# Squares added by VectorE, two query products between the output projection's last jobs, and one paced list for the weight and inner sums

## The chip, the cores and the metric

The kernel runs on one core of a Trainium2 chip. The metric is the device time of one execution in microseconds (us), median of the runs. The core's engines are PE (TensorE, matrix products), DVE (VectorE), ACT (ScalarE), POOL (GpSimd) and SP (SyncE, which here only issues transfers). ACT and POOL issue transfers as well. Each engine works through its own instructions in order and waits on semaphores for the others.

## The reference

One decoder layer on 1024 tokens of width 1024: a state-space branch and an mLSTM branch, merged by gates and projected; cross-attention into 256 memory tokens; a ConvFFN; a final norm. Cut to what the change touches:

```python
merged = g_s5 * (y_s5 @ w_br_s5) + g_m * (y_m @ w_br_m)
x = x + merged @ w_out                                   # output projection
h = _rmsnorm(x, x_norm_g)                                # needs the squares of x
x = x + _cross_attn(h, _rmsnorm(mem, mem_norm_g), wq, wkv, wo)
h = _rmsnorm(x, f_norm_g)
u = _causal_dwconv(h @ w_up, conv_w, conv_b)             # up projection, 1024 -> 2 x 2816
a, b = split(u, 2)
x = x + (gelu(a) * b) @ w_down
return _rmsnorm(x, final_norm_g)
```

## The kernel before

**Products.** Activations lie with channels on the partitions. Every float32 product is made of three matmuls on a high and a low part of each operand (high x high, high x low, low x high). A weight tile is loaded by SP into a raw buffer, cast to its high part by ACT (L187) and subtracted to its low part by DVE (L188); `load_w` (L193) does this. The raw buffers WR and the parts WH and WL have two buffers each.

**Seven products for eight.** The gates, output, query, up and down projections are cut into 2 x 2 blocks and done with seven block products (numbered 1 to 7) in place of eight, by Winograd's form of Strassen's method. Some of the seven need sums of weight blocks. These are made in DRAM by transfers that POOL issues, half of them plain copies and half with an adding write: `quad_sums` (L982) yields eight transfers for a piece (512 KB each, smaller ones for the odd last piece of the down weights). The weight sums are Gw (gates), Ow (output), Qw (query), Uq (first eight pairs of the up projection) and Dd (down). They stand in one list, `slow_sums`, 120 entries in this order. `next_sum` (L210) issues the next one and makes it wait for the latest matmul (`last_mm`); `sums_on` sets how often a call does so: 0 never, 1 at each call, n when the argument is a multiple of n. The down projection also needs sums of the inner activations, Td from Gq, 40 entries, which `hidden_sums` (L1555) issues eight at a time as soon as pairs 8, 10, 12, 15 and 17 are finished, the first four of each eight waiting for the latest up product.

**Stages around the change.** First come the branches and gates, in an order written by hand (`ORDER`, L51), where `SUMS_OFF` and `SUMS_HALF` name the steps with no sums or half of them. The output projection has 14 jobs (`ojobs`, L1028): block products 1, 2, 3, 6, 7, 5, 4, each for two column groups. `out_job` (L1076) asks for the next job's weights, for the residual of the job after it, does 24 matmuls, calls `next_sum`, and empties PSUM; `out_x` (L1057) makes the new x from a result, its split for the query product, its squares on ACT, and adds them to `sq1` on POOL (L1069). No sums are issued in this stage, since `sums_on` is 0. The residual of jobs 12 and 13 comes by loads of POOL, the second of each adding (L1052, L1053).

The query stage follows a list (`QKV`, L62): j is a query product (14 of them, `q_job`, L1190, 24 matmuls), k a tile of keys, v a step of the values, s and t sums and splits of x for later query products, x the norm of x, a the first scores. Query products 0 and 1 need only the parts of x that output jobs 2 and 3 make; 2 and 3 need those of jobs 10 and 11, 4 and 5 those of jobs 12 and 13. Products 12 and 13 are kept for the attention (`Q_LATE`).

The attention has eight units (two token halves, four heads): scores, softmax, transposes, values (L1699 to L1716). From unit 4 on the tiles of the product with w_o run in between. Its first weight tile is asked for in unit 4. Some of the softmax tiles take WR buffers (L1309).

The up projection has 154 jobs of 12 matmuls (L1668, L1669): for pairs 0 to 7 first products 1 and 2 (jobs 0 to 15), then five each (jobs 16 to 55), then seven for each of pairs 8 to 21. Pairs 0 to 7 load sums from Uq, Y tiles of 256 KB; later pairs load two halves of 512 KB (`in_w_up`, L1479) and add the blocks on DVE (L1483). A finished pair goes through convolution and gelu, and is stored in Gq or Gd. The down projection has 63 jobs of 12 matmuls, and then a last part for the last four pairs.

**Order.** The program text gives priorities; a planner puts the instructions of each engine in order by a simulated timeline, so that an instruction may stand ahead of others that are earlier in the text. On the chip each engine keeps the order that was planned.

Of the kernel before, what the change touches and what calls it, by code (L numbers as in the profile page):

```python
# [15 lines left out]
ALU = mybir.AluOpType  # L16
# [4 lines left out]
P = 128  # L21
T = 1024
D = 1024
KD = D // P
# [29 lines left out]
).split()  # L54
NG = 2
SUMS_OFF = "p2 r1 g0 l2 y0 a1 l3 r2 r3 e10 e11 e20 e21 e30 e31 e60".split()
SUMS_HALF = ("a0", "a2", "a3", "a4")

Q_SUM = range(14)
Q_LATE = {0: 12, 2: 13}  # L60
V_FROM = 1
QKV = (  # L62
    "j0 s0 j1 k0 s1 v0 s2 j2 s3 k1 v1 t60 j3 t61 k2 t62 v2 t63 j4 x0 k3 t70 v3 t71 j5 k4 t72 v4 t73 j6 k5 t40 v5 t41 j7 t42 k6 v6 t43 j8 k7 v7 t50 j9 t51 t52 t53 j10 j11 a0 a1 "
).split()

COLS = {}
# [25 lines left out]
def hybrid_layer(ctx: ExitStack, tc: tile.TileContext, a):  # L92
    nc = tc.nc
# [963 lines left out]
    def out_x(n, h, u, ps):  # L1057
        i, odd = n // 2, n % 2
        x = qraw[i, odd, h] = Y() if odd or h else qe0[i // 2][:, H[i % 2]]
        V.tensor_tensor(out=x, in0=u, in1=ps, op=ALU.add)  # L1060
        if odd or not h:
            t = (S if odd else VV)(F32R)
            qp[1 + odd + odd * h, i] = scaled_split(x, col("x_g", n) if odd == h else nxg[:, n : n + 1], t[:, H[0]], t[:, H[1]])
        if fresh_sq[h]:
            A.activation(out=sq1[h], in_=x, func=AF.Square)
        else:
            t = Y()
            A.activation(out=t, in_=x, func=AF.Square)
            G.tensor_tensor(out=sq1[h], in0=sq1[h], in1=t, op=ALU.add)  # L1069
        fresh_sq[h] = False  # L1070
        A.dma_start(out=X1d[n][:, H[h]], in_=x)

# [2 lines left out]

    def out_job(k):  # L1076
        p, g = ojobs[k]
        out_weights(k + 1)
        out_resid(k + 2)
        wh, wl = ows.pop((p, g))  # L1080
        if p != 2:
# [196 lines left out]
    for k, (p, g) in enumerate(ojobs):  # L1278
        if k in (1, 2):
            out_sums(2 * k - 2)  # L1280
        if k in OUT_TURNS:
            out_turn(OUT_TURNS[k])
        if k == MEM_AT:
            mem_parts()
        out_job(k)

    r2s = cp.tile([P, 8], F32, name="r2s")
    r2n = cp.tile([P, 8], F32, name="r2n")
# [99 lines left out]
            nc.sync.dma_start(out=t, in_=X1d[n])  # L1388
            x1.append(t)

    def o_load(n):
        ow.append(load_w(a["w_o"][n % KD], (KD, P)))

    def o_tile(half, n):
        hs = H[half]
# [157 lines left out]
    Td = dr.tile([NPP, P, 4, T], F32, name="Td")  # L1553

    def hidden_sums(jj):  # L1555
        for i, (out, in_, kw) in enumerate(quad_sums(Td, Gq, jj, (1, 3, 3, 2), (0, 1, 0, 2), both_of(jj), range(8))):
            d = nc.gpsimd.dma_start(out=out, in_=in_, **kw)
            if i < 4:
                tc.add_manual_dep(d.ins, up_mm[0].ins.name, DependencyInfo(DependencyClass.Sync, DependencyReason.DATA), reason="pace")

    up_mm = [None]

# [134 lines left out]
    turned = None  # L1697
    sums_on[0] = 1
    for u in range(len(units)):  # L1699
        if u == 4:  # L1700
            o_load(0)
            x1_load(0)
            x1_load(1)
        probs(u + 1, 0)
        if u in Q_LATE:
            q_job(Q_LATE[u])
        elif u < 4:
            next_sum()
        t_ = att_turn(pes.pop(u))
        first_half(2 * (u - 5) + 1)  # L1710
        probs(u + 1, 1)
        if u:
            att_values(*units[u - 1], turned)
            next_sum()
        turned = t_
        first_half(2 * (u - 4))  # L1716
    first_half(KD - 1)
    att_values(*units[-1], turned)
    for n in range(KD):
        if n < KD - 1:  # L1720
            o_load(n + 1)
        o_tile(1, n)
        if n < 6:
            next_sum()
        if n == 1:
            pb = o_norm(0)
# [48 lines left out]
        put(4, i, xo[:, H0], S)  # L1775
    for i in range(4):
        put(3, i, x1[2 * i + 1][:, H1], S)
    raws, ops, wraws = [iter(range(len(djobs))) for _ in range(3)]
    for k in range(2 * NE, len(jobs)):
        up_job(k)  # L1780
        i = k - (len(jobs) - 7)
        if i >= 0:
# [18 lines left out]
    gs, ws = [], []  # L1801
    for k in range(len(djobs)):
        down_job(k)
        down_wraw(next(wraws, len(djobs)))
        down_w(k + 7)
        down_raw(next(raws, len(djobs)))
# [179 lines left out]
```

## Time and profile before

| | us |
|---|---|
| median of three runs | 1617.1 |
| lowest, highest | 1613.93, 1621.98 |
| the profiled execution | 1621.01 |
| its span, first to last instruction | 1619.2 |

PE's granted clock was 0.991 of full speed in the mean. The chain of work that ended last, followed back from the last instruction, by engine:

| engine or wait | share of the span |
|---|---|
| PE | 79% |
| DVE | 8% |
| DMA | 7% |
| ACT | 4% |
| issue | 2% |

How to read it: a row of the timeline with [idle <- releaser] gives how long the engine stood before this instruction and what it waited for last. Matmuls are pipelined: the duration of one overlaps the next. The share of busy time is a mean over stages with different limits, so stages are read one by one, in windows. In rows of the windows the last three numbers are the granted clock, the busy share of the 16 DMA engines and GB/s.

The stages in the profiled execution: output projection to about 680 us, query stage to about 800, attention and product with w_o to about 950, up projection to 1388, down projection after it.

### The profile page before, as it was taken

The page shows a single profiled execution, that of the slowest core. Times are in us where ns is not written, and L with a number is a line of the kernel's source. Part 1 is how long each engine was busy: PE and PEld are TensorE (multiplying, and loading weights), DVE is VectorE, ACT ScalarE, POOL GpSimd, SP SyncE. Part 2 cuts the span into 40 slices and gives each one's busy share as a digit, 9 for nine tenths or more (in the row PEclk, how much of TensorE's full clock was granted, in tenths as well). Part 3 has the DMA queues.
Part 4 walks back from the last instruction along what each step waited for, and adds up shares of the span by engine and source line. Part 5 has one row for each costly group of instructions (what it writes and reads, how often), then busy time and mean ns, then how long its engine had stood idle before and what let it go on. Part 6 is the DMA issues. An engine that isn't in the chain of part 4 may idle for free.

```text
span 1619.2 us, 21148 instructions
## 1 busy us (share of the span) xinstructions
PE 1575.9 (97%) x7887; PEld 1323.6 (82%) x7887; DVE 1168.5 (72%) x1844; ACT 772.6 (48%) x1261; POOL 206.8 (13%) x288
## 2 busy tenths in 40 slices
PE   9999999999999999899989999999989999999997
PEld 7898888888888787788878877888877888888887
DVE  7878767675565897957676558789877978967535
ACT  6446555633564447644454336444443444643413
POOL 1001111000101102410010100000121011221014
PEclk9999999999999999999999999999999999999998
DMA  6255645645986667565475568754797466876312
GB/s 200 94 148 136 157 118 126 149 98 143 294 300 179 147 156 227 176 205 175 106 225 147 168 184 267 202 153 127 213 228 181 123 176 200 310 262 207 119 39 105
DMA packets 104391, 282.09 MB, mean 174 GB/s; under 512 B 11488, under 2 KB 25504, under 8 KB 104288
## 3 DMA queue, kind: packets, MB, share of 16 engines
q1 hardware_dynamic: 67456, 163.90, 30.3%
q0 software_dynamic: 29296, 102.51, 28.1%
q10 hardware_dynamic: 7536, 14.33, 2.3%
q8 instruction: 62, 1.02, 0.3%
q14 instruction: 41, 0.34, 0.1%
HBM read 245.57 MB, written 114.82 MB: 223 GB/s over the span
## 4 chain that ended last, share of the span: by engine, by line
PE 79%; DVE 8%; DMA 7%; ACT 4%; issue 2%; POOL 0%; ACTq 0%; POOLq 0%; SPq 0%; DVEq 0%
PE M L223 25%; PE A L1505 11%; PE M L1505 9%; PE M L1652 6%; PE A L1652 5%; PE A L895 4%; PE M L1200 4%; PE A L223 2%; DMA S<-in_w_up_dram 2%; PE A L1267 1%; PE M L310 1%; DMA WR<-in_w_uq_dram 1%; PE A L1372 1%; DVE WL L188 1%; ACT S L187 1%
## 5 line engine op out<-in xcount | busy, mean ns | idle before, releaser
L223 PE MATMUL M<-S,WH 128*128 128x512 f32 (+1 forms) x1160 | 312.2, 380 | 5.8 <-ACT WH L187 4.0
L223 PEld LDWEIGHTS M<-S,WH 128*128 128x128 f32 x1160 | 211.6, 189 | 45.8 <-ACT WH L187 4.6
L187 ACT CAST WH<-WR 128x1024 fp32r<-128x1024 f32 (+2 forms) x113 | 107.4, 950 | 223.0 <-PE M L223 83.8
L223 PE MATMUL M<-S,WL 128*128 128x512 f32 (+1 forms) x580 | 184.3, 378 | 1.3 <-DVE WL L188 1.3
L188 DVE TENSOR_TENSOR WL<-WR,WH 128x1024 fp32r<-128x1024 f32 (+2 forms) x113 | 126.1, 1116 | 47.6 <-ACT WH L187 46.4
L223 PEld LDWEIGHTS M<-S,WL 128*128 128x128 f32 x580 | 109.1, 189 | 21.6 <-DVE WL L188 2.2
L1505 PE MATMUL M<-S,Y 128*128 128x512 f32 x468 | 111.9, 389 | 0.0
L1505 PEld LDWEIGHTS M<-S,Y 128*128 128x128 f32 x468 | 87.8, 188 | 18.5 <-DVE Z L1518 0.3
L1528 DVE SCALAR_TENSOR_TENSOR S<-Z,cols,S 128x1023 f32<-128x1023 f32 (+1 forms) x72 | 90.6, 1278 | 7.8 <-ACT S L1526 7.6
L1505 PE MATMUL M<-S,W 128*128 128x512 f32 x324 | 78.3, 389 | 0.0
L187 ACT CAST W<-Y 128x512 fp32r<-128x512 f32 x51 | 31.4, 619 | 85.8 <-PE A L1505 62.0
L1505 PE MATMUL A<-S,W 128*128 128x512 f32 x288 | 70.9, 389 | 0.7 <-ACT W L187 0.7
L1505 PEld LDWEIGHTS M<-S,W 128*128 128x128 f32 x324 | 60.8, 188 | 12.6
L1092 PE MATMUL A<-S,WH 128*128 128x512 f32 x224 | 69.0, 396 | 1.2 <-ACT A L1086 0.7
L895 PE MATMUL A<-S,WH 128*128 128x512 f32 x224 | 67.2, 390 | 0.0
L1505 PE MATMUL A<-R,W 128*128 128x512 f32 x228 | 58.3, 400 | 7.1 <-ACT Z L1512 7.1
L1505 PEld LDWEIGHTS A<-S,W 128*128 128x128 f32 x288 | 54.0, 188 | 12.2 <-ACT W L187 1.1
L1505 PE MATMUL A<-S,Y 128*128 128x512 f32 x240 | 59.9, 389 | 0.0
L188 DVE TENSOR_TENSOR S<-S,S 128x512 fp32r<-128x512 f32 x79 | 52.3, 685 | 9.8 <-ACT S L187 9.6
L1200 PE MATMUL M<-S,WH 128*128 128x512 f32 x192 | 59.3, 390 | 0.0
L1505 PEld LDWEIGHTS A<-R,W 128*128 128x128 f32 x228 | 43.6, 192 | 17.6 <-ACT Z L1512 8.4
L1652 PE MATMUL M<-S,W 128*128 128x512 f32 x240 | 57.7, 389 | 0.0
(528 smaller groups left out, 3594.4 us busy)
## 6 DMA issues: line engine op xcount, KB each, us to landing
Uq<-in_w_uq_dram POOLq DMA_DIRECT2D x24, 512.0 KB, 4.9
Dd<-in_w_dq_dram POOLq DMA_DIRECT2D x24, 512.0 KB, 5.8
Td<-Gq POOLq DMA_DIRECT2D x24, 512.0 KB, 8.1
WR<-in_w_in_dram SPq DMA_DIRECT2D x21, 512.0 KB, 4.3
Gq<-S SPq DMA_DIRECT2D x18, 512.0 KB, 4.3
WR<-in_w_o_dram SPq DMA_DIRECT2D x16, 512.0 KB, 4.5
Y<-Uq SPq DMA_DIRECT2D x32, 256.0 KB, 5.2
S<-Td POOLq DMA_DIRECT2D x16, 512.0 KB, 5.3
```

Of the source, the lines that this page charges most:

```text
L187: A.copy(out=hi, in_=src)
L188: (lo_eng or V).tensor_tensor(out=lo, in0=src, in1=hi.bitcast(F32), op=ALU.subtract)
L223: last_mm[0] = PE.matmul(ps[:, s:e], lhsT, rhs[:, s:e], start=first and is_first, stop=last and is_last)
L310: PE.matmul(pus[j][h.start // 512], w_[:, 0, j * P : (j + 1) * P], x_[:, h], start=k == 0 and f, stop=k == KD - 1 and l)
L895: last_mm[0] = PE.matmul(ps[q], w[:, 0, c], x, start=f, stop=l, skip_group_check=True)
L1092: last_mm[0] = PE.matmul(ps[q], w[:, 0, c], x, start=f, stop=l, skip_group_check=True)
L1200: last_mm[0] = PE.matmul(ps[q], w[:, 0, c], x, start=f, stop=l)
L1267: PE.matmul(pv[2 * m + j], lhsT, rhs[:, 0, 512 * j : 512 * j + 512], start=k == 0 and f, stop=k == KD - 1 and l)
L1372: last_mm[0] = PE.matmul(po, lhsT[:, ns], rhs, start=f, stop=l)
L1505: up_mm[0] = PE.matmul(ps, lhsT[:, c], rhs, start=f, stop=l, skip_group_check=True)
L1528: V.scalar_tensor_tensor(out=acc[:, d_:], in0=raw[:, : T - d_], scalar=col("fcw", 3 * ct + 2 - d_), in1=acc[:, d_:], op0=ALU.mult, op1=ALU ...
L1652: paced[0] = PE.matmul(dps[p][n], lhsT[:, c], rhs, start=f, stop=l, skip_group_check=True)
```

## The change

Six things are edited. (1) The squares of x are added by VectorE instead of GpSimd. (2) Query products 0 and 1 are moved from the head of the query list to between output jobs 11, 12 and 13; their weights are asked for in jobs 11 and 12 (`OUT_Q`), and value weights are asked for from the first step of the query stage on. (3) One sum is issued in every odd output job (and by the second of the moved products), two more in gate tiles a2 and a3, fewer in the attention's second half and beside the product with w_o. (4) Query product 12 runs in unit 1 of the attention, not in unit 0. (5) The first weight tile of w_o is asked for in unit 3, into a Z buffer in place of a WR buffer. (6) The inner sums go to the end of `slow_sums`, and the up projection issues one sum every fourth job before job 28 and one every second job from there on; the down jobs would issue what is left.

```diff
-SUMS_HALF = ("a0", "a2", "a3", "a4")
+SUMS_HALF = ("a0", "a4")
 
 Q_SUM = range(14)
-Q_LATE = {0: 12, 2: 13}
-V_FROM = 1
+Q_LATE = {1: 12, 2: 13}
+V_FROM = -1
+OUT_Q = {11: 0, 12: 1}
 QKV = (
-    "j0 s0 j1 k0 s1 v0 s2 j2 s3 k1 v1 t60 j3 ...
+    "s0 j2 s1 k0 s2 v0 s3 k1 v1 t60 j3 ...
@@ out_x
-            G.tensor_tensor(out=sq1[h], in0=sq1[h], in1=t, op=ALU.add)
+            V.tensor_tensor(out=sq1[h], in0=sq1[h], in1=t, op=ALU.add)
@@ out_job
-        out_weights(k + 1)
+        if k in OUT_Q:
+            q_weights(OUT_Q[k])
+        else:
+            out_weights(k + 1)
@@ the loop over the output jobs
+        sums_on[0] = k % 2
+        if k - 1 in OUT_Q:
+            out_weights(k)
+            q_job(OUT_Q[k - 1])
         out_job(k)
+    sums_on[0] = 0
@@ o_load
-    def o_load(n):
-        ow.append(load_w(a["w_o"][n % KD], (KD, P)))
+    def o_load(n, raw=None):
+        ow.append(load_w(a["w_o"][n % KD], (KD, P), raw=raw))
@@ hidden_sums
-        for i, (out, in_, kw) in enumerate(quad_sums(Td, Gq, jj, (1, 3, 3, 2), (0, 1, 0, 2), both_of(jj), range(8))):
-            d = nc.gpsimd.dma_start(out=out, in_=in_, **kw)
-            if i < 4:
-                tc.add_manual_dep(d.ins, up_mm[0].ins.name, DependencyInfo(DependencyClass.Sync, DependencyReason.DATA), reason="pace")
+        slow_sums.extend(quad_sums(Td, Gq, jj, (1, 3, 3, 2), (0, 1, 0, 2), both_of(jj), range(8)))
@@ the units of the attention
+        if u == 3:
+            o_load(0, Z())
         if u == 4:
-            o_load(0)
             x1_load(0)
             x1_load(1)
         probs(u + 1, 0)
         if u in Q_LATE:
             q_job(Q_LATE[u])
-        elif u < 4:
-            next_sum()
...
         if u:
             att_values(*units[u - 1], turned)
-            next_sum()
+            if u < 4:
+                next_sum()
@@ second half of the product with w_o
-        if n < 6:
+        if n in (1, 3, 5):
             next_sum()
@@ the up jobs
+    UP_SUMS = 28
     for k in range(2 * NE, len(jobs)):
+        sums_on[0] = 4 if k < UP_SUMS else 2
         up_job(k)
@@ the down jobs
         down_job(k)
+        last_mm[0] = paced[0]
+        for _ in range(0 if k < 2 else len(slow_sums)):
+            next_sum()
+        next_sum()
```

More of the change, by code (lines that the diff above doesn't have):

```diff
@@ L56 @@
 SUMS_OFF = "p2 r1 g0 l2 y0 a1 l3 r2 r3 e10 e11 e20 e21 e30 e31 e60".split()
-SUMS_HALF = ("a0", "a2", "a3", "a4")
+SUMS_HALF = ("a0", "a4")
 Q_SUM = range(14)
-Q_LATE = {0: 12, 2: 13}
-V_FROM = 1
+Q_LATE = {1: 12, 2: 13}
+V_FROM = -1
+OUT_Q = {11: 0, 12: 1}
 QKV = (
-    "j0 s0 j1 k0 s1 v0 s2 j2 s3 k1 v1 t60 j3 t61 k2 t62 v2 t63 j4 x0 k3 t70 v3 t71 j5 k4 t72 v4 t73 j6 k5 t40 v5 t41 j7 t42 k6 v6 t43 j8 k7 v7 t50 j9 t51 t52 t53 j10 j11 a0 a1 "
+    "s0 j2 s1 k0 s2 v0 s3 k1 v1 t60 j3 t61 k2 t62 v2 t63 j4 x0 k3 t70 v3 t71 j5 k4 t72 v4 t73 j6 k5 t40 v5 t41 j7 t42 k6 v6 t43 j8 k7 v7 t50 j9 t51 t52 t53 j10 j11 a0 a1 "
 ).split()
```

## The prediction

> **What bounds the kernel now.** The reading goes from the page's table of engines, through the timeline of PE (only rows with an idle time in brackets), to the granted clock around the longer gaps. Rows of the timeline give start, duration, engine, line, operation, count and [idle before, releaser]; rows of the windows give busy time and instructions of each engine, then PEclk, DMA share and GB/s.
>
> ```profile
> PE 1575.9 (97%) x7887; PEld 1323.6 (82%) x7887; DVE 1168.5 (72%) x1844; ACT 772.6 (48%) x1261; POOL 206.8 (13%) x288
> ...
> 630.19 0.50 PE L1092 MATMUL A<-S,WL 128*128 128x512 f32 x1 [1.13 <-DVE WL L188]
> 663.95 0.73 PE L1092 MATMUL A<-S,WH 128*128 128x512 f32 x2 [0.74 <-ACT A L1086]
> 666.58 0.79 PE L1092 MATMUL A<-S,WL 128*128 128x512 f32 x1 [1.89 <-DVE WL L188]
> 681.76 0.50 PE L1200 MATMUL M<-VV,WL 128*128 128x512 f32 x1 [2.50 <-DVE WL L188]
> 833.41 1.01 PE L223 MATMUL M<-S,WH 128*128 128x512 f32 x2 [3.70 <-ACT WH L187]
> 962.84 4.62 PE L1505 MATMUL A<-R,Y 128*128 128x512 f32 x12 [1.96 <-ACT Z L1512]
> 1198.00 2.61 PE L1505 MATMUL A<-R,W 128*128 128x512 f32 x7 [4.37 <-ACT Z L1512]
> 1254.09 0.50 PE L1505 MATMUL A<-R,W 128*128 128x512 f32 x1 [2.50 <-ACT Z L1512]
> ```
>
> PE is busy for 1575.9 of 1619.2 us, and the change takes no matmul away. It can only win idle time of PE, and what idle time costs afterwards. Five places matter: the end of the output projection (0.74 + 1.89), the start of the query stage (2.50), the attention (3.70), the start of the up projection (1.96) and its middle (4.37 + 2.50).
>
> ```profile
> 663.00:670.00 7.00, 4.37 (x11) 3.02 (x11) 7.00 (x7) 4.73 (x8) 5.03 (x4) 0.76 0.44 130
> 832.00:838.00 6.00, 4.50 (x13) 3.18 (x14) 4.58 (x7) 4.05 (x8) 0.00 (x0) 0.72 0.69 180
> 962.00:968.00 6.00, 5.16 (x18) 4.16 (x19) 2.15 (x4) 2.91 (x6) 1.03 (x1) 0.72 0.29 94
> 1190.00:1204.00 14.00, 9.63 (x36) 7.45 (x35) 12.86 (x18) 6.35 (x9) 3.29 (x4) 0.88 0.88 187
> 1250.00:1256.00 6.00, 3.50 (x16) 2.58 (x15) 6.00 (x9) 3.73 (x6) 0.62 (x2) 1.00 0.90 208
> ```
>
> Four of the gaps are followed by a slower clock: (1 - 0.76) x 7, (1 - 0.72) x 6, again that, and (1 - 0.88) x 14 are 1.7 us lost each. The gap at 1254 lost none (clock 1.00).
>
> The Trainium skill, page "TensorE: Matmul & The Clock Gate", Part 1, says that the clock falls to half after an idle window of about 3.4 us; by that rule the gaps of 1.96 and of 0.74 + 1.89 would cost no clock, and the forecast would come out 1.7 us later (the clock behind the second pair, counted below). The rows 663 and 962 show the loss behind both, so the measurement decides.
>
> **The change part by part.** The sum goes against the profiled execution, 1621.0 us (span 1619.2 and 1.8 around it). It is 3.9 above the median of 1617.1.
>
> *Output projection and query stage.* The rows are groups by form in 650 to 692 (count | busy, mean ns), then a query product on the chain of waits.
>
> ```profile
> L188 DVE TENSOR_TENSOR WL<-WR,WH 128x1024 fp32r<-128x1024 f32 x7 | 10.7, 1524 | 0.5 <-ACT WH L187 0.5
> L1060 DVE TENSOR_TENSOR Y<-S,A 128x512 f32<-128x512 f32 x12 | 8.0, 678 | 0.0
> L1171 DVE SCALAR_TENSOR_TENSOR Y<-Y,nxg,Y 128x512 f32<-128x512 f32 x4 | 4.9, 1221 | 1.5 <-ACT Y L1170 1.5
> L1173 DVE TENSOR_TENSOR R<-R,Y 128x512 f32<-128x512 f32 x4 | 4.8, 1204 | 0.0
> L1174 DVE SCALAR_TENSOR_TENSOR Y<-Y,cols,R 128x512 f32<-128x512 f32 x4 | 3.0, 741 | 0.0
> L188 DVE TENSOR_TENSOR VV<-Z,VV 128x1024 fp32r<-128x1024 f32 x1 | 1.2, 1214 | 0.0
> L1069 POOL TENSOR_TENSOR Z<-Z,Y 128x512 f32<-128x512 f32 x14 | 21.6, 1543 | 36.2 <-ACT Y L1068 36.1
> 692.70 5.44 PE M L1200 x24
> ```
>
> The 14 POOL adds (21.6 us) go; DVE gets them at about 0.68 each (L1060, the same shape): 14 x 0.68 = 9.5 us more. DVE also gets something back: while POOL adds, like operations are stretched, L1171 from 0.741 (L1174) to 1.221, L1173 from 0.678 to 1.204, L188 from 1.214 to 1.524: 4 x 0.48 + 4 x 0.53 + 7 x 0.31 = 6.2 us. Net 3 us more on an engine that is full here (7.00 of 7.00 in row 663). That is covered by the moved products. Products 0 and 1 (5.44 each, 24 matmuls) need only the evictions of jobs 2 and 3, long done, and their result leaves through ACT; between jobs 11, 12 and 13 they give DVE 10.9 us to bring the next weights. So the gaps 0.74 + 1.89 and their 1.7 of clock should go. What is late next is the first product after job 13, now product 2, with its low weight half behind the last evictions: I leave half of 2.50. Gain 0.74 + 1.89 + 1.7 + 1.25 = 5.6. The bounds are 0 (DVE decides as before) and 6.8 (all of it). Each moved product brings its 512 KB load on SP's queue, one job ahead as the out loads were; no load is added.
>
> Seven sums now run beside the out jobs, where none ran.
>
> ```profile
> q0 software_dynamic: 29296, 102.51, 28.1%
> ...
> 590.00:680.00 90.00, 84.53 (x360) 67.03 (x359) 76.53 (x104) 62.02 (x105) 26.75 (x23) 0.98 0.63 190
> 1037.00:1114.00 77.00, 77.00 (x342) 63.75 (x341) 68.77 (x87) 34.92 (x44) 4.89 (x7) 1.00 0.57 165
> 1114.00:1388.00 274.00, 267.13 (x1170) 220.10 (x1169) 222.30 (x297) 119.60 (x174) 40.05 (x61) 0.99 0.69 186
> ```
>
> POOL's queue moved 102.51 MB in 28.1% of the span, 4.4 us of all 16 engines per MB, so a 512 KB sum is about 2.3 us (my estimate from that row). Seven add 16 us to 90 us at 0.63: 0.81. A sum waits for an out job's matmul, and behind it on POOL stand the residual loads of jobs 12 and 13 (L1052, L1053) and the power of the memory norm; ACT's copy at L1086 waits for those loads. They have two jobs and a product as cover. Cost between 0 and 7.4 (two stalls like that at 962, 3.7 with its clock); I take 1.5.
>
> *Attention.* The rows are ACT's waits in 826 to 835 and SP's queue.
>
> ```profile
> ACT WH L187 <- DMA WR<-in_w_o_dram: 6.2, 1, 6.2
> 823.66 11.31 SPq L196 DMA_DIRECT2D WR<-in_w_o_dram  x3
> ```
>
> The first weight tile of w_o waits until 823.66 for a WR buffer that softmax holds; ACT stands 6.2 us on its cast, with exponentials queued behind. In a Z buffer and a unit earlier the load is out of the way, and fewer sums run beside it. Gain 3.70 + 1.7 = 5.4 (from 1.7, if the next tile is late instead by 3.70, up to 5.4). Product 12 a unit later leaves unit 0 less cover: cost between 0 and 3.7 (the same gap again), 1.0 taken.
>
> *Start of the up projection.*
>
> ```profile
> 952.75 0.80 POOL L214 DMA_DIRECT2D Dd<-Dd  x1 [12.53 <-PE A L1505]
> 961.69 0.62 ACT L187 CAST Y<-WR 128x512 fp32r<-128x512 f32 x1 [5.72 <-DMA WR<-in_w_uq_dram]
> ```
>
> An adding sum starts at 952.75, and ACT stands 5.72 us for a weight load. Sums beside the second half of the output product go from six to three, but counted through the list an adding one still falls here, four jobs later. Of 1.96 + 1.7 I take 1.0; bounds 0 and 3.7.
>
> *One list in the up projection.* The rows are the chain of waits, medians to landing, and POOL's queue.
>
> ```profile
> 1157.84 10.65 DMA S<-in_w_up_dram
> 1173.96 7.33 DMA Gq<-S
> 1181.31 9.64 DMA S<-in_w_up_dram
> ...
> S<-in_w_up_dram SPq DMA_DIRECT2D x14, 512.0 KB, 4.3
> Gq<-S SPq DMA_DIRECT2D x18, 512.0 KB, 4.3
> ...
> 1176.71 2.07 POOL L1557 DMA_DIRECT2D Td<-Gq  x4 [2.54 <-PE M L1505]
> 1202.97 0.82 POOL L214 DMA_DIRECT2D Dd<-in_w_dq_dram  x1 [0.25 <-issue]
> ```
>
> Three transfers that stand behind one another are 6.35, 3.03 and 5.34 later than their medians, 14.7 in all, beside a burst of inner sums; PE waits 4.37, so about 10 us are absorbed. In the new list each sum waits for its own job, one per two jobs. Counted through, 47 sums fall after job 56 where 53 fell. Without bursts I expect the three less than 10 us late: the gaps 4.37 and 2.50 and 1.7 of clock go, gain 8.6 (bounds 0 and 8.6). The price stands earlier: jobs 28 to 55 carry 14 sums instead of 7, so 16 us more in 77 us at 0.57: 0.78. That stage had no gap (77.00 of 77.00), so the cost lies between 0 and six stalls like that at 1198 (6.1 with its clock) for six pairs, 36; I take 2.0, as 0.78 is nearer the row 1114 (0.69, 7 us lost in 274, most of it behind bursts) than a full queue.
>
> The rest costs nothing: two more sums in the gate tiles a2 and a3 come out of later places, v weights asked for earlier fill buffers that product 0 and 1 now free earlier, and the list is empty by job 148 of 154, so that the calls in the down stage find nothing.
>
> Sum: 1621.0 - 5.6 + 1.5 - 5.4 + 1.0 - 1.0 - 8.6 + 2.0 = 1604.9. I take **1605**, and hold it for the median too: the 3.9 us of the profiled execution are most likely more of the transfer waits that go.
>
> **The rivals.**
> 1. *The up projection keeps half its waits*: row 1114 stays near 0.69 whatever the order, and adding sums still meet a pair's three transfers. Half of 8.6 stays: 1609. Against it: both gaps stand behind bursts.
> 2. *DVE decides at the seam*, and the products move the gaps only: 1605 + 5.6 = 1611. For it: 7.00 of 7.00 in row 663.
> 3. *The change doesn't do what it says* in the order of the engines: instructions are put in order by a planner, and products and sums may land elsewhere. Both seam and start of the up stage gain nothing, 1605 + 5.6 + 1.0 = 1612.
> 4. *Late start of the down stage.* The rows are POOL's first load for it, and the stage's first matmuls.
>
> ```profile
> 1354.84 0.59 POOL L1581 DMA_DIRECT2D S<-Gq  x1 [4.61 <-DVE Y L188]
> 1388.09 21.53 PE M L1652 x95
> ```
>
> If the last sums stand ahead of these loads in POOL's queue, 33 us of lead shrink to a few: one stall of 6.1, 1611.
> 5. *Slower*: the doubled rate in jobs 28 to 55. Sums and the loads of Y from Uq collide, the place decides as soon as loads come more than a pair (five products, 13.6 us) late, and each of six pairs stalls 6.1: 1605 - 2 + 36.6 = 1639; with half of the pairs 1621. Against it: share 0.78, and no gap there before.
>
> The Trainium skill, page "Trainium Kernel Development and Optimization", Key Constraints, says that transfers from SP's, ACT's and POOL's queues interleave on the same 16 DMA engines. By that rule a list that only moves sums frees nothing and shifts the waits, which is rivals 1 and 5; the 9.64 beside 4.3 in the rows above agrees.
>
> **How the numbers follow.** Forecast 0.56 (own range 1597 to 1610, the bounds of the small costs), rivals 1 to 5: 0.13, 0.09, 0.08, 0.06, 0.08. The range is 1594 (all the gains, no cost: 1621.0 - 6.8 - 5.4 - 3.7 - 8.6 = 1596.5, and 2.5 for the spread of the runs) to 1620, which leaves rival 5 out and a few mixtures. A measurement of this kernel tells about 0.5% from no change: 1609.0 and 1625.2 are the bounds. Faster: 0.48 of the forecast's 0.56 and half of rival 1 and some of the others, 0.60; slower 0.08; the same 0.32.
>
> **What would show it.** Right: no PE gap over 1 us before jobs 12 and 13 and none at the cast of w_o; L1173 near 0.68; no gap over 1 us in jobs 56 to 153, and medians of S<-in_w_up near 4.3. Wrong: gaps behind Y<-Uq loads in jobs 28 to 55, late out loads from Ow, a gap at the first down job, or a new one at unit 0 of the attention; each names its rival.

## Result and profile after

| kernel | median us (lowest to highest) | runs |
|---|---|---|
| before, beside it | 1621.57 (1613.93 to 1629.26) | 20 |
| changed | 1612.34 (1606.78 to 1617.3) | 20 |

The ratio is 0.9946, 95% interval 0.9933 to 0.9959: 9.2 us or 0.54% faster. The profiled execution took 1610.45 us, its span is 1608.7. The 20 runs of the kernel before have their median at 1621.57, so its profiled execution (1621.01) was an ordinary one and the median of the first three runs was low.

Where the 10.5 us between the two spans lie is read from the first and last start of the matmuls on each stage's lines:

| stage, us | before | after |
|---|---|---|
| up to the first out job | 582.1 | 581.1 |
| output projection and query stage (first out job to last query product) | 224.9 | 225.1 |
| attention (to its last values) | 96.1 | 91.7 |
| rest of the product with w_o | 46.5 | 46.4 |
| up projection (first to last matmul) | 438.1 | 433.7 |
| from there to the end | 231.5 | 230.7 |

The attention and the up projection gave 4.4 us each, the seam between output projection and query stage nothing, though most of the edits are there. The last query product is number 13, which runs in unit 2 of the attention, so this stage holds the attention's first units too; to the end of product 11 it takes 206.3 us before and 207.2 after, the same picture. The rest, 1.0 and 0.8, lies in stages that the change touches little. The page's table of engines of the changed kernel, and then the rows of PE's timeline with an idle time (in brackets, with its releaser), answer the first rows of before:

```profile
PE 1576.2 (98%) x7887; PEld 1324.3 (82%) x7887; DVE 1169.6 (73%) x1858; ACT 774.2 (48%) x1261; POOL 185.8 (12%) x274
```

```profile
628.95 0.56 PE L1096 MATMUL A<-S,WL 128*128 128x512 f32 x1 [1.14 <-DVE WL L189]
665.65 1.21 PE L1096 MATMUL A<-S,WH 128*128 128x512 f32 x4 [2.08 <-ACT WH L188]
667.97 0.79 PE L1096 MATMUL A<-S,WL 128*128 128x512 f32 x1 [1.10 <-DVE WL L189]
831.16 0.73 PE L224 MATMUL M<-S,WH 128*128 128x512 f32 x2 [0.33 <-ACT WH L188]
1203.43 2.08 PE L1514 MATMUL A<-R,W 128*128 128x512 f32 x4 [3.81 <-ACT Z L1521]
```

The gaps of 2.50 at the first query product, 3.70 at the cast of w_o (now 0.33), 1.96 at the start of the up projection and 2.50 at 1254 are gone. The pair 0.74 + 1.89 before the last out jobs is now 2.08 + 1.10, and 4.37 in the middle of the up projection is 3.81. Behind both the clock drops; rows of the windows (third number from the end is the granted clock, then DMA share and GB/s):

```profile
628.00:640.00 12.00, 11.05 (x42) 8.97 (x43) 11.57 (x19) 7.80 (x15) 5.78 (x9) 0.86 0.83 218
663.00:675.00 12.00, 8.81 (x26) 6.39 (x25) 11.44 (x17) 8.98 (x14) 0.00 (x0) 0.72 0.49 158
1195.00:1212.00 17.00, 13.19 (x46) 10.09 (x45) 12.12 (x17) 4.23 (x7) 1.35 (x2) 0.80 0.71 204
1037.00:1114.00 77.00, 77.00 (x340) 63.49 (x339) 67.08 (x84) 33.22 (x41) 10.07 (x15) 1.00 0.70 185
1114.00:1385.00 271.00, 266.62 (x1162) 219.64 (x1161) 224.14 (x299) 123.95 (x181) 36.98 (x56) 0.99 0.68 181
```

(1 - 0.72) x 12 and (1 - 0.80) x 17 are 3.4 us each. With the gaps ahead of them the two places cost 6.6 and 7.2 us. The gap of 1.14 at 628.95 was there before (1.13 at 630.19), but now it costs another (1 - 0.86) x 12 = 1.7 us of clock. The same window of before shows none:

```profile
628.00:640.00 12.00, 10.87 (x48) 8.67 (x48) 12.00 (x21) 9.15 (x18) 4.15 (x6) 1.00 0.65 174
```

**The seam after.** The groups by form between 650 and 692 us (count | busy, mean ns | idle before):

```profile
L189 DVE TENSOR_TENSOR WL<-WR,WH 128x1024 fp32r<-128x1024 f32 x7 | 8.5, 1221 | 4.4 <-ACT WH L188 4.4
L1061 DVE TENSOR_TENSOR Y<-S,A 128x512 f32<-128x512 f32 x12 | 8.0, 680 | 0.0
L1070 DVE TENSOR_TENSOR Z<-Z,Y 128x512 f32<-128x512 f32 x10 | 6.8, 685 | 0.3 <-ACT Y L1069 0.3
L1175 DVE SCALAR_TENSOR_TENSOR Y<-Y,nxg,Y 128x512 f32<-128x512 f32 x4 | 3.0, 749 | 3.0 <-ACT Y L1174 3.0
L1177 DVE TENSOR_TENSOR R<-R,Y 128x512 f32<-128x512 f32 x4 | 2.7, 684 | 0.0
```

With GpSimd's adds gone, VectorE's operations are no longer stretched: the subtraction takes 1.221 us where it took 1.524, L1177 0.684 where it took 1.204, L1175 0.749 where it took 1.221. But VectorE now waits for ScalarE (3.0 and 4.4 us of idle time). ScalarE's own rows, from its timeline:

```profile
641.86 1.05 ACT L188 CAST WH<-WR 128x1024 fp32r<-128x1024 f32 x1 [4.20 <-DMA WR<-Ow]
648.95 1.05 ACT L188 CAST WH<-WR 128x1024 fp32r<-128x1024 f32 x1 [3.99 <-DMA WR<-Ow]
656.54 0.72 ACT L1174 ACTIVATE Y<-Y,nxg 128x512 f32<-128x512 f32 x1 [1.41 <-DMA X1d<-Y]
656.61 0.81 ACTq L1072 DMA_DIRECT2D X1d<-Y  x2
662.81 0.72 ACT L1174 ACTIVATE Y<-Y,nxg 128x512 f32<-128x512 f32 x1 [3.10 <-DMA X1d<-Y]
664.57 1.03 ACT L188 CAST WH<-WR 128x1024 fp32r<-128x1024 f32 x1
```

L1174 scales a half of the new x in place, so it must wait until the store of that half (L1072, to X1d) has landed. ScalarE works in order: while the first L1174 waits, two stores stand behind it and go out together at 656.61; the second L1174 waits for one of them until 662.81, and the cast of the next out job's weights (664.57) stands behind that. PE waits 2.08 for it. Ahead of this, two casts already waited 4.20 and 3.99 us for weight loads from Ow.

**The up projection after.** POOL's rows of the timeline ahead of the gap at 1203, and then the chain of waits there:

```profile
1179.61 0.81 POOL L215 DMA_DIRECT2D Td<-Td  x1 [10.74 <-PE M L1514]
1189.15 0.81 POOL L215 DMA_DIRECT2D Td<-Td  x1 [8.73 <-DMA Td<-Td]
1189.80 0.71 POOL L215 DMA_DIRECT2D Td<-Gq  x1
1193.35 0.53 POOL L215 DMA_DIRECT2D Td<-Gq  x1 [2.85 <-PE M L1514]
```

```profile
1180.82 9.12 DMA Gq<-S
1189.96 8.58 DMA S<-in_w_up_dram
```

The sums are paced by the jobs, but one that adds to the result of the one just ahead of it waits 8.73 us for it, and the sums due meanwhile then follow closely (1189.15, 1189.80, 1193.35): a burst again. Beside it the store of a finished tile (9.12) and the load into its buffer (8.58) stand one behind the other, where the medians of the whole run are 5.6 and 4.0.

### The profile page after: what moved, and what is told of

Same layout as the page of the kernel before. It is cut to its first block, busy times and chain, and to the rows that moved or that the text cites. A ratio compares the mean times of both kernels' runs of the same rounds, so it can differ in the third digit from the quotient of the medians.

```text
span 1608.7 us, 21174 instructions
## 1 busy us (share of the span) xinstructions
PE 1576.2 (98%) x7887; PEld 1324.3 (82%) x7887; DVE 1169.6 (73%) x1858; ACT 774.2 (48%) x1261; POOL 185.8 (12%) x274
## 4 chain that ended last, share of the span: by engine, by line
PE 81%; DMA 7%; DVE 6%; ACT 3%; issue 2%; POOL 0%; ACTq 0%; POOLq 0%; SPq 0%; DVEq 0%
PE M L224 24%; PE A L1514 12%; PE M L1514 9%; PE M L1658 6%; PE A L1658 5%; PE A L896 4%; PE M L1204 4%; PE A L224 4%; PE A L1096 2%; PE A L1271 1%; PE M L311 1%; DMA Gq<-S 1%; DVE S L1537 1%; PE A L1381 1%; PE A L1314 1%
## 5 line engine op out<-in xcount | busy, mean ns | idle before, releaser
L189 DVE TENSOR_TENSOR WL<-WR,WH 128x1024 fp32r<-128x1024 f32 (+2 forms) x112 | 122.8, 1097 | 44.2 <-ACT WH L188 42.8
L188 ACT CAST S<-S 128x512 fp32r<-128x512 f32 x79 | 46.5, 618 | 22.0 <-DVE S L189 8.9
```

What stands on the lines that cost most here:

```text
L188: A.copy(out=hi, in_=src)
L189: (lo_eng or V).tensor_tensor(out=lo, in0=src, in1=hi.bitcast(F32), op=ALU.subtract)
```

## Experiments

All are compared with the kernel before on the same chip (medians 1619.8, 1620.36, 1622.07 and 1622.63 in the four sets). Stage lengths are from one profiled execution each; single executions spread by some 5 us up or down, so only differences of several us in a stage are read.

| kernel | median us | ratio (95%) | seam | attention | up |
|---|---|---|---|---|---|
| before | 1621.57 | 1 | 224.9 | 96.1 | 438.1 |
| changed | 1612.34 | 0.9946 (0.9933 to 0.9959) | 225.1 | 91.7 | 433.7 |
| e1_squares_pool | 1611.14 | 0.9941 (0.9921 to 0.9962) | 225.8 | 92.0 | 431.8 |
| e2_products_head | 1624.77 | 1.0028 (1.0012 to 1.0044) | 225.8 | 96.6 | 448.4 |
| e3_attention_back | 1610.25 | 0.9937 (0.9919 to 0.9956) | 223.9 | 95.5 | 429.5 |
| e4_list_back | 1607.59 | 0.9915 (0.9899 to 0.9932) | 223.8 | 92.6 | 432.5 |
| e5_head_and_list_back | 1624.9 | 1.0029 (1.0013 to 1.0045) | 228.2 | 95.1 | 438.5 |
| e6_no_store_wait | 1604.71 | 0.9912 (0.9893 to 0.9932) | 218.8 | 92.0 | 434.3 |
| e7_sums_spread | 1607.46 | 0.9923 (0.9905 to 0.9942) | 225.9 | 91.9 | 426.5 |
| e8_rate_tripled | 1610.53 | 0.9948 (0.993 to 0.9966) | 225.1 | 91.7 | 430.3 |
| e9_fresh_and_spread | 1600.1 | 0.9867 (0.984 to 0.9895) | 217.6 | 94.6 | 431.3 |
| e10_only_products | 1613.68 | 0.9953 (0.9935 to 0.9971) | 220.7 | 93.9 | 438.3 |
| e11_no_late_sums | 1618.94 | 0.9991 (0.9969 to 1.0013) | 224.9 | 93.0 | 441.5 |
| e12_products_and_squares | 1609.42 | 0.9901 (0.9869 to 0.9933) | 219.9 | 94.0 | 441.8 |

### One part of the change undone at a time

**The squares on GpSimd again.**

```diff
-            V.tensor_tensor(out=sq1[h], in0=sq1[h], in1=t, op=ALU.add)
+            G.tensor_tensor(out=sq1[h], in0=sq1[h], in1=t, op=ALU.add)
```

> The changed kernel with the squares added by GpSimd again (part 1 undone). Theory A (the two engines hinder each other): DVE operations with two SBUF inputs are stretched again, L1177 from 0.68 to about 1.2 us, the gaps at the seam (3.2 us before the last output jobs) grow by 2 to 4 us, ratio to the kernel before 0.996 to 0.997. Theory B (ACT, which stands at L1174 until a store to X1d has landed, decides at the seam): DVE is stretched all the same, but the gaps stay at 3 to 4 us and the ratio at 0.9946.

Measured: 0.9941, not to be told from the changed kernel's 0.9946. VectorE is stretched again (L1177 takes 1.073 us, between 650 and 692), and the time stays, as theory B had it. In the complete change this edit is worth nothing: the engine that it relieves of stretching is not the one that is late.

**The products at the head of the query list again.**

```diff
-V_FROM = -1
-OUT_Q = {11: 0, 12: 1}
+V_FROM = 1
+OUT_Q = {}
-    "s0 j2 s1 k0 s2 v0 s3 ...
+    "j0 s0 j1 k0 s1 v0 s2 j2 s3 ...
```

> The changed kernel with query products 0 and 1 back at the head of the query list (part 2 undone). Theory A (the products cover the seam): a gap of 2 to 3 us comes back at the first query product, and those at the last output jobs grow, ratio 0.996 to 0.998. Theory B (the products only move the gaps, as DVE and ACT are late by the same): the gaps from 640 to 700 us sum to 3 to 5 us as in the changed kernel (3.2), ratio 0.9946.

Measured: 1.0028, 0.8% behind the changed kernel. The seam is only 0.7 us longer, but the attention takes 4.9 and the up projection 14.7 us more. The planner's order differs on all engines from the seam on, so this one edit also moved what meets in the up projection.

**The attention's edits undone.**

```diff
-Q_LATE = {1: 12, 2: 13}
+Q_LATE = {0: 12, 2: 13}
-        if u == 3:
-            o_load(0, Z())
         if u == 4:
+            o_load(0)
```

> The changed kernel with the first w_o tile in unit 4 and a WR buffer, and query product 12 in unit 0 again; the sums stay thinned. Theory A (the WR buffer held by the softmax is the cause): the gap of 3 to 4 us before the first w_o product comes back with its slower clock, 5 us more, ratio 0.998. Theory B (the sums beside the load were the cause): the load takes 4 to 5 us instead of 8.6, the gap is 1 us or less, ratio 0.995.

Measured: 0.9937. The attention is 3.8 us longer, the up projection 4.2 us shorter, and the time the same within its interval. The gap at the cast of w_o comes back as 1.35 us, not as the 3 to 4 of theory A, so the WR buffer alone did not make the 3.70 of before.

**The bursts of inner sums again, weight sums one in four jobs all through.**

```diff
-        slow_sums.extend(quad_sums(Td, Gq, jj, ..., range(8)))
+        for i, (out, in_, kw) in enumerate(quad_sums(Td, Gq, jj, ..., range(8))):
+            d = nc.gpsimd.dma_start(out=out, in_=in_, **kw)
+            if i < 4:
+                tc.add_manual_dep(d.ins, up_mm[0].ins.name, ..., reason="pace")
...
-        sums_on[0] = 4 if k < UP_SUMS else 2
```

> The changed kernel with the inner sums issued in bursts of eight again and one weight sum every fourth job all through the up projection (part 6 undone). Theory A (bursts cause the late transfers): gaps of 2 to 5 us behind a pair's load come back, two of them or more in 1114 to 1390, 3 to 6 us in all more than the 3.8 of the changed kernel, ratio 0.997 to 0.998. Theory B (the chain from the store of a pair to the next load is late under either order): one to two gaps, 4 to 7 us in all, ratio 0.9946 to 0.996.

Measured: 0.9915, faster than with the one list; the intervals 0.9899 to 0.9932 and 0.9933 to 0.9959 just part (only four runs of this kernel). Both theories had it slower than that. The bursts leave a gap of 3.55 near 1204 as the list leaves 3.81. The list as built gained nothing.

### Products and list together

```diff
-OUT_Q = {11: 0, 12: 1}
+OUT_Q = {}
...
-        sums_on[0] = 4 if k < UP_SUMS else 2
```

> Both the products' place and the bursts of inner sums as in the kernel before; squares on VectorE, the attention's first w_o tile and the sums beside the out jobs stay as changed. Theory A (the moved products win by themselves, whatever the list is; the two parts add): the products were worth 0.82% (1.0028 against 0.9946) and the list costs 0.31% (0.9946 against 0.9915), so a ratio of 1.0028 - 0.0031 = 0.9997, about no change, and PE waits in the up projection as before (a gap of 3 to 4 us near 1200, another of 1 to 3 near 1254). Theory B (the products' place only matters because with them at the head the list's doubled rate meets loads that stand late): without the list the place is worth little, ratio 0.991 to 0.994, and the matmuls from the first up job to the last take 431 to 435 us. The up stage tells them apart: 448 us in the kernel with only the products at the head, 434 in the changed one.

Measured: 1.0029, the up projection 438.5. So with the products at the head the change is no gain with either list. Neither theory had the sizes: moving the products is worth 0.8% with the list (1.0028 to 0.9946) and 1.1% without it (1.0029 to 0.9915), and the list's price is at most 0.3% and not seen here, although the up projection was 10 us shorter without it. At the seam, with the sums beside the out jobs and the products not between them, there is a longer stall than the kernel before had:

```profile
669.88 0.79 PE L1096 MATMUL A<-S,WH 128*128 128x512 f32 x1 [5.09 <-ACT A L1090]
```

### What is late at the seam

**A fresh buffer in place of the scaling in place.**

```diff
-        for e, g_ in ((e0, col("x_g", n - 1)), (e1, nxg[:, n - 1 : n])):
-            A.activation(out=e, in_=e, func=AF.Copy, scale=g_)
+        f1 = Y()
+        A.activation(out=f1, in_=e1, func=AF.Copy, scale=nxg[:, n - 1 : n])
+        A.activation(out=e0, in_=e0, func=AF.Copy, scale=col("x_g", n - 1))
+        e1 = qraw[i, 0, 1] = f1
```

Only the second half, e1, gets the fresh buffer; it is now scaled first, and e0 behind it, still in place.

> The scaled half of x goes into a fresh buffer, so ScalarE's scaling no longer waits for the store of x. Theory A (this wait, 3.10 us at 662.81 in the changed kernel, is what is late at the seam): the gaps of 2.08 and 1.10 before the last out jobs go or fall under 1 us together, the clock there is over 0.9, the stretch from the first out job to the last query product takes 221 to 223 us where it took 225.1, and the ratio falls by 0.0015 to 0.003, to 0.9915 to 0.993. Theory B (the whole seam is bound by the sum of work on VectorE and ScalarE, the wait is cover for work that would come anyway): the gaps stay over 2 us together, releaser VectorE or ScalarE with no wait for a DMA ahead of it, and the stretch takes 224.5 to 225.5; ratio 0.994 to 0.995.

Measured: 0.9912, the seam 218.8 us, 6.3 shorter. Two rows of the windows of this kernel, and then one of ScalarE's timeline:

```profile
650.00:668.00 18.00, 18.00 (x85) 14.99 (x84) 16.81 (x25) 13.77 (x22) 1.59 (x2) 1.00 0.85 249
663.00:675.00 12.00, 12.00 (x55) 9.94 (x54) 10.74 (x15) 8.07 (x12) 0.02 (x1) 1.00 0.88 262
```

```profile
649.59 1.05 ACT L188 CAST WH<-WR 128x1024 fp32r<-128x1024 f32 x1 [5.50 <-DMA WR<-Ow]
```

PE is busy 12.00 of 12.00 us at full clock where the changed kernel had 8.81 at 0.72. Theory A holds: the wait on the store was the stall. A cast waits 5.50 us for its load here, and PE does not stall behind it.

**The kernel before with the moved products alone.** The earlier value weights (`V_FROM`) and the shorter query list go with them.

```diff
+OUT_Q = {11: 0, 12: 1}
...
+        if k - 1 in OUT_Q:
+            out_weights(k)
+            q_job(OUT_Q[k - 1])
         out_job(k)
```

> The kernel before with the two query products between the last out jobs and nothing else of the change: squares on GpSimd, no sums beside the out jobs, bursts of inner sums and the attention as before. Theory A (the products win at the seam by themselves and the sums beside the out jobs take it back): the stretch from the first out job to the last query product takes 219 to 222 us where it took 224.9, with gaps under 1.5 us in all before the last out jobs, and the ratio is 0.993 to 0.996. Theory B (ScalarE's wait for the store of x is late there with or without those sums): the stretch takes 223.5 to 226 us, gaps of 2 to 4 us in all before the last jobs, ratio 0.996 to 1.000.

Measured: 0.9953, seam 220.7, as theory A had them, though the gaps before the last jobs, 1.28 and 1.41, are larger than its 1.5 in all. The wait for the store at this place is 0.15, as its row shows (a later one, at 668.76, is 1.79):

```profile
659.79 0.72 ACT L1174 ACTIVATE Y<-Y,nxg 128x512 f32<-128x512 f32 x1 [0.15 <-DMA X1d<-Y]
```

The one edit gives nearly the whole gain of the six (0.9946): 4.2 us at the seam and 2.2 in the attention, where the gap at the cast of w_o falls from 3.70 to 1.41 without the edits that were meant for it. The gaps of 1.96 at the start of the up projection and of 2.50 at 1254 are gone here too, without the edits to the sums.

**The changed kernel without sums in out jobs 9 to 13.**

```diff
-        sums_on[0] = k % 2
+        sums_on[0] = k % 2 if k < 9 else 0
...
-        if n in (1, 3, 5):
+        if n in (1, 3, 5, 6):
...
-    UP_SUMS = 28
+    UP_SUMS = 16
```

> The changed kernel without the sums beside out jobs 9 to 13 (they go into the output product and the up projection). Theory A (those sums are what makes the store of x land late): ScalarE's wait of 3.10 us at the seam falls under 1.5 us, the gaps of 2.08 and 1.10 fall under 1.5 together, the stretch from the first out job to the last query product takes 221 to 223 us where it took 225.1, and the ratio is 0.991 to 0.9935. Theory B (the loads of weights and residuals that run there anyway make it late, as in the kernel before with its 2.69 us): the wait stays over 2.3 us, the stretch takes 224 to 225.5, ratio 0.994 to 0.996.

Measured: 0.9991, seam 224.9, ScalarE's wait 3.97. The late sums are not the cause of the wait; the ratio is worse than either theory had it. The up projection, whose doubled rate begins 12 jobs earlier here, takes 7.8 us more.

**The moved products and the squares, no sums beside the out jobs.**

```diff
-            G.tensor_tensor(out=sq1[h], in0=sq1[h], in1=t, op=ALU.add)
+            V.tensor_tensor(out=sq1[h], in0=sq1[h], in1=t, op=ALU.add)
```

> The kernel with only the two moved products, and the squares added by VectorE besides; still no sum beside the out jobs. On ScalarE the order near the last out jobs changes with it: the scaling that waits for a store then stands ahead of the next piece's square and store. Theory A (the squares, with the place that the planner gives to ScalarE's scaling, bring back the wait): ScalarE waits 2.5 to 4 us for the store of x, gaps of 2.5 to 4.5 us in all before the last out jobs, the stretch from the first out job to the last query product takes 224 to 226 us where only the products took 220.7, ratio 0.997 to 1.000. Theory B (the sums beside the out jobs bring it back): the wait stays under 1 us, the stretch takes 219 to 221.5 us, ratio 0.993 to 0.996.

Measured: 0.9901, seam 219.9. Half of each theory came: the wait is back (3.50, as A had it), and the stretch is as short as B had it. This kernel's rows from ScalarE's timeline, to be laid beside those of the changed one, and then of the kernel without the late sums one of POOL and one of ScalarE:

```profile
641.26 1.05 ACT L188 CAST WH<-WR 128x1024 fp32r<-128x1024 f32 x1 [2.73 <-DMA WR<-Ow]
646.61 1.05 ACT L188 CAST WH<-WR 128x1024 fp32r<-128x1024 f32 x1 [2.25 <-DMA WR<-Ow]
661.04 0.72 ACT L1174 ACTIVATE Y<-Y,nxg 128x512 f32<-128x512 f32 x1 [3.50 <-DMA X1d<-Y]
```

```profile
635.40 1.11 POOL L215 DMA_DIRECT2D Uq<-Uq  x1
```

```profile
649.80 1.05 ACT L188 CAST WH<-WR 128x1024 fp32r<-128x1024 f32 x1 [4.20 <-DMA WR<-Ow]
```

ScalarE does the same operations in the same order from 636 to 667 us in these three kernels. Where an adding sum (one that adds to what stands in DRAM) goes out at 635.40 or 635.68 (out job 7), the last load from Ow lands late and its cast stands at 649.80 and 648.95; with no sum it stands at 646.61. The view of transfers of 636 to 668 us (last number: us from issue to landing) has for the changed kernel and then for this one

```profile
WR<-Ow SPq DMA_DIRECT2D x1, 512.0 KB, 10.7
```

```profile
WR<-Ow SPq DMA_DIRECT2D x1, 512.0 KB, 7.5
```

So by these traces the early sums take 2 to 3 us of ScalarE's lead, and the wait of 3 to 4 us for the store, most of which that lead would have covered, reaches PE: gaps of 1.01 + 1.12 at full clock without the sums, 2.08 + 1.10 or 4.27 with them, and both of these with 3.4 us of clock lost behind. The slower clock is thus more of the price than the longer gaps are. No run takes the early sums alone out of the changed kernel. But all fourteen kernels agree: this load from Ow lands after 9.3 to 11.1 us in the eleven with early sums, and after 7.0 to 8.0 in the three without.

### What is late in the up projection

**The eight sums of a piece in another order.** Only POOL's queue differs from the changed kernel.

```diff
-        slow_sums.extend(quad_sums(..., range(8)))
+        slow_sums.extend(quad_sums(..., (0, 2, 4, 1, 6, 3, 5, 7)))
```

> The eight sums of a piece in an order in which no sum stands right behind the one that it needs; nothing else moves on any engine but on GpSimd's queue. Theory A (sums that wait for one another bunch up and the bunch meets the pair's store and load: four sums within 11 us from 1189.80 in the changed kernel, and PE's gap of 3.81 at 1203): GpSimd's waits for another sum (8.73 at 1189.15) go, the gap near 1203 falls under 2 us, the up projection takes 430 to 432 us where it took 433.7, ratio 0.992 to 0.9935. Theory B (the serial pair of a store and the load into its buffer decides, with whatever is on the queue): the gap stays between 3 and 5 us, the up projection takes 433 to 435, ratio 0.994 to 0.9955.

Measured: 0.9923 (its interval overlaps that of the changed kernel a little), up projection 426.5 us, 7.2 shorter, the gap gone. By the ratios it is 3.7 us; the profiled execution was the fastest of its six. POOL's timeline of this kernel, and then two of its windows:

```profile
1175.51 0.83 POOL L215 DMA_DIRECT2D Td<-Td  x1 [6.67 <-PE A L1514]
1179.52 0.82 POOL L215 DMA_DIRECT2D Td<-Gq  x1 [3.17 <-PE M L1514]
1189.11 0.54 POOL L215 DMA_DIRECT2D Td<-Gq  x1 [8.77 <-PE A L1514]
```

```profile
1114.00:1371.00 257.00, 256.45 (x1131) 212.01 (x1130) 218.96 (x293) 118.72 (x174) 35.90 (x54) 1.00 0.70 184
1195.00:1212.00 17.00, 17.00 (x77) 14.08 (x76) 14.22 (x20) 8.75 (x13) 1.35 (x2) 1.00 0.66 178
```

Between 1175 and 1208 POOL waits for jobs (PE) here, not for another sum, and PE is busy 17.00 of 17.00 where it was 13.19. The DMA share is 0.70 where it was 0.68: as many bytes moved, at other times. So the share alone does not stall this stage. What the traces suggest is a meeting: an adding sum beside a store and the load into the stored buffer. The wait behind a predecessor is not enough for it: with the old order GpSimd also waits 7.43 us at 1171.91 in e8_rate_tripled and 9.01 at 1200.94 in e11_no_late_sums, and PE has no gap over 1 us near either.

**One sum per job in up jobs 28 to 55.**

```diff
-        sums_on[0] = 4 if k < UP_SUMS else 2
+        sums_on[0] = 4 if k < UP_SUMS else 1 if k < 56 else 2
```

> One sum per job in up jobs 28 to 55 where the changed kernel has one per two jobs and the kernel before one per four; as many sums in all. Theory A (the rate beside the pieces of Y from memory is a cost as soon as stores stand behind it, as in the kernel with the products at the head, where 5 us of gaps fell between 1040 and 1115): the list is empty earlier, but the stretch of these jobs gets gaps of 3 to 15 us in all, its share of DMA stays at 1.00 and the landing of S<-in_w_up or Gq<-S in it is over 8 us; ratio 0.996 to 1.004. Theory B (that stretch has room: PE was busy 77.00 of 77.00 there): no gap over 1 us in it, fewer sums in the stage behind it, whose gap of 3.81 shrinks; ratio 0.992 to 0.995.

Measured: 0.9948. The window of jobs 28 to 55 in this kernel:

```profile
1041.00:1118.00 77.00, 76.67 (x339) 63.14 (x338) 65.84 (x83) 33.16 (x42) 12.63 (x18) 1.00 0.77 201
```

No stall there at twice the rate of the changed kernel, and the gap near 1203 is gone (up projection 430.3). Theory B holds for this kernel. Yet two others stalled in the same stretch: with the products at the head, PE was busy 68.70 of 75.00 us, and with the doubled rate from job 16 on, 73.52 of 77.00. A row of ScalarE and PE's row behind it in the first of them, and then the chain of waits in the second:

```profile
1063.02 0.62 ACT L188 CAST Y<-Y 128x512 fp32r<-128x512 f32 x1 [4.15 <-DMA Y<-Uq]
1065.15 0.72 PE L1514 MATMUL M<-S,W 128*128 128x512 f32 x2 [2.91 <-ACT W L188]
```

```profile
1087.12 7.12 DMA Gq<-S
1099.89 5.59 DMA S<-in_w_up_dram
```

The first is the mechanism of the slow rival: ScalarE waits for a load of Y from Uq, and the cast that PE needs stands behind it. In the second it is a store and the load of up weights behind it (PE's gap is 3.48 at 1108.10). The doubled rate alone sets off neither, as the window above, at one sum per job, shows; that it depends on which transfers meet is the likely reading, and no run isolates it.

### The two repairs together

The edits of e6_no_store_wait and e7_sums_spread on the changed kernel, in their core:

```diff
+        f1 = Y()
+        A.activation(out=f1, in_=e1, func=AF.Copy, scale=nxg[:, n - 1 : n])
...
+        slow_sums.extend(quad_sums(..., (0, 2, 4, 1, 6, 3, 5, 7)))
```

> The fresh buffer for the scaled half of x and the spread order of the sums together, on the changed kernel. Theory A (the two stalls lie in different stages and add): out projection and query about 219 us, up projection about 427 us, ratio about 0.9912 + 0.9923 - 0.9946 = 0.989, time 1600 to 1603. Theory B (an earlier start of the up projection shifts what meets there, and a gap at a store and its load comes back): up projection 430 to 434 us, ratio 0.991 to 0.992.

Measured: 0.9867, median 1600.1 of six runs (one of them, 2249.74 us, is left out of the ratio; the others lie between 1595.68 and 1608.63). It is the fastest version, some 12 us ahead of the changed kernel, and the two gains add (0.989 was expected, and the interval is 0.984 to 0.9895). Its profiled execution was the slowest of the five, 8.5 us over the median, and began its first out job 5.1 us later than the changed kernel did; its 431.3 in the up projection is therefore no measure of the median run. The gap that theory B expected did not come back in it: near 1203 PE stands 0.86 and 0.62 us, and its longest gap in the stage is 1.63, at 989.75.

## Why the prediction came out as it did

The forecast was 1605 and the range 1594 to 1620; 1612.3 lies inside. But the gain is 9.2 us where 16.1 were summed up (1621.0 to 1604.9), and of the sum's two largest terms, the seam and the middle of the up projection, little came; that the total fell into the range is in part luck. The first step rests on a row of ScalarE's timeline before:

```profile
659.82 0.72 ACT L1170 ACTIVATE Y<-Y,nxg 128x512 f32<-128x512 f32 x1 [2.69 <-DMA X1d<-Y]
```

By its own steps:

1. **Output projection and query stage (-5.6, +1.5): the seam gave +0.2.** This is the step that failed, in its term for the sums. The moved products do win there: 4.2 us alone and 5.0 with the squares, against 5.6 forecast. The stretching by GpSimd's adds and its end were read rightly (L1177 0.684). But the sums beside the out jobs cost 225.1 - 219.9 = 5.2 us, not 1.5 (the same without the late ones: 224.9 - 219.9 = 5.0); the bounds of 0 to 7.4 held it. These are differences between kernels that differ in later stages too. The mechanism was another than the one priced: I looked at POOL's queue and the residual loads behind a sum, while by the traces the sum of job 7 made the last weight load from Ow late ("late out loads from Ow" stood among the signs of being wrong), and ScalarE lost the lead that covered its wait for the store of x. That wait was in the trace of before too (2.69 us at 659.82, the row above) and I did not use it: I asked what VectorE has behind the last evictions, and not what ScalarE has. Rival 2 had the size (no gain at the seam), with the wrong engine. The row of 14 adds on GpSimd in the prediction is of the whole stage; between 650 and 692 there are 11.
2. **Attention (-5.4 + 1.0): measured -4.4.** The number came, the reasons only in part. Counted from the end of product 11, so that product 12 is in it, the stage gave 5.1: the gap at the cast of w_o with its clock, and no cost of product 12. The products alone shrink this gap to 1.41, so the Z buffer is not its only cause; and with the edits undone the 3.8 us that the attention loses come back in the up projection. What a stall here is worth at the end of the program was not as sure as the sum made it.
3. **Start of the up projection (-1.0).** The gap of 1.96 went entirely, and no slow clock follows it (956 to 968: 1.00): 3.7 rather than 1.0, the upper bound. The thinner sums that the term was given for are not shown to be the cause, as the gap is gone with the products alone too (e10_only_products).
4. **Middle of the up projection (-8.6).** Of 4.37 + 2.50 + 1.7 of clock, 8.6 in all, 3.81 + 3.4 stayed or came anew. This is rival 1. The reason given was that one sum per two jobs makes no bursts; the trace shows a burst behind a sum that waited for its predecessor, and in e7_sums_spread, where only POOL's order differs, the gap is gone. The 2.50 at 1254 did go, but it also goes with the bursts as they were (e10_only_products). As built, the list is not faster than the bursts (e4_list_back).
5. **Doubled rate in jobs 28 to 55 (+2.0): measured 0** (77.00 of 77.00 busy, DMA share 0.70 where 0.78 was forecast). Stalls in that stretch came in two experiments, at 3.5 and 6.3 us of idle time; in the second of these the trace shows rival 5's own mechanism (e2_products_head).
6. **The time around the span.** Holding the forecast against the profiled execution for the median too was right only by luck: the three runs' median was low, and in 20 runs it is 1621.6. The reason given, more of the waits that go, was not it.

Rival 3 (the planner places things elsewhere) was no rival but a condition of every experiment: moving the products at the seam changed the up projection by 14.7 us (e2_products_head). So single edits cannot be priced by their own stage alone, and the shares of the six edits in the 9.2 us are not to be had by undoing them one by one. What is shown: the products alone give nearly the whole gain, and the wait for the store of x is what stalls PE at the seam of the changed kernel. That the early sums bring this stall about rests on the comparison of all kernels. The order of the sums in the list holds back 4 to 7 us by the ratios (0.9946 to 0.9923, and 0.9912 to 0.9867 with the fresh buffer), in both pairs with intervals that still overlap a little.

What stays open: the kernel with the products and the squares alone has the second-best ratio (0.9901), ahead of the complete change, and half a per cent ahead of the products alone (0.9953; the intervals just part), while undoing the squares in the complete change costs nothing. Its profile shows no stage that would account for it: seam 219.9 against 220.7, up projection 441.8 against 438.3. Its profiled execution was the slowest of its six runs (1613.2 against a median of 1609.4), so that the stage lengths hide part of the answer.

## What to carry to other kernels

Before an engine is relieved at a seam, list what every engine in the chain of that seam waits for, with its slack: a wait of 3 us that is covered before the change can be the bound after it. An operation in place on a tile that is being stored waits for the store, and on an engine that works in order it holds back the next stores and casts too; a fresh buffer took the stall away here (6.3 us at the seam). A paced list of transfers stays paced only if no entry waits for the one just ahead of it, so order it by dependence first and set its rate second.

## What the runs showed of the hardware

- GpSimd's adds stretch only some of VectorE's operations: L1177, with both inputs in SBUF, takes 0.684 us without them and took 1.204 beside them, while L1061 (L1060 before), which reads a PSUM tile, takes 0.680 and took 0.678. With the adds on GpSimd again (e1_squares_pool) L1177 takes 1.073 and L1061 0.679.
- The loss of clock behind a gap doesn't follow the gap's length. The gap of 1.14 at 628.95 lost 1.7 us in the changed kernel, and a gap of 1.13 there none in the kernel before. In the kernel without the late sums a window of 12 us behind a gap of 2.87 lost 1.7 us (0.86), and behind 2.08 + 1.10 the changed kernel lost 3.4 (0.72). In the kernel with products and squares alone a gap of 3.32 lost none. The window of the first of these, then PE's row and the window of the last:

```profile
994.00:1006.00 12.00, 11.49 (x44) 9.39 (x45) 9.70 (x16) 5.53 (x10) 0.54 (x1) 0.86 0.88 249
```

```profile
1204.88 3.06 PE L1512 MATMUL M<-S,Y 128*128 128x512 f32 x12 [3.32 <-DVE Z L1525]
```

```profile
1204.00:1216.00 12.00, 11.12 (x49) 9.18 (x50) 11.14 (x18) 5.18 (x7) 2.09 (x4) 1.00 0.68 158
```
